# A two-block transformer trunk on one core: seven-product pairs in the last product, attention outputs kept on chip, the last two gate tiles plain

## The chip, the cores and the metric

One core of one Trainium2 chip runs the whole program. The metric is device time in microseconds (us), the median of the runs of one kernel; one further execution is profiled. TensorE (PE in the rows, with its weight loads as PEld) multiplies, VectorE (DVE) and ScalarE (ACT) do elementwise work, GpSimd (POOL) does elementwise work and issues software DMAs, SyncE (SP) issues most of the other DMAs.

## The reference, cut to what matters

Everything is f32 with 512 tokens and a model width of 2048. The first block has two layers; each is a norm, one wide input product, two kinds of attention side by side, a gate, an output product and a residual. The second block has one layer with 16 extra tokens ahead, a stick-breaking attention, a pooling branch, two sigmoid gates and an output product, and a last norm.

```python
for l in range(2):                                   # first block
    h = rmsnorm(x, attn_norm_g[l]);  proj = h @ w_in[l]
    ya = swa_attention(qa, ka, va, sinks) * silu(ga)    # 16 heads of 64, window 128
    yb = mla_attention(cq, ckv, kr, ...) * silu(gb)     # 8 heads, value width 128
    x = x + concat([ya, yb]) @ w_out[l]
x = rmsnorm(x, final_norm_g)
# second block, on meta tokens + x
zin = rmsnorm(x) @ w_in_2      # q, k, v, g_attn, u, g_pool, m_attn, m_pool
merged = sigmoid(m_attn) * (o_attn @ w_attn_up) + sigmoid(m_pool) * (o_pool @ w_pool_up)
out = rmsnorm(x + merged @ w_out_2)
```

## The kernel before, in words

Activations lie transposed: a tile is 128 features by 512 tokens, and a width of 2048 is 16 tiles. Each f32 operand is split into two fp32r parts, a high one (`split`, a ScalarE cast) and a low one (a VectorE subtraction, both in lines 133 to 139), and each product is three matmuls, high by high, high by low and low by high (`mm3`, line 152). The same is done to each weight block: `w_raw` (line 178) loads 128x1024 f32 by a DMA of SyncE into one of four `wr` buffers, and `load_w_split` (line 215) makes `wh` on ScalarE and `wl` on VectorE, three buffers each. `next_w` (line 222) keeps two split blocks ahead. A plain output tile takes two blocks and 96/2 = 48 matmuls of 512 columns. `run_gemm` (line 281) runs one tile, or a group of three, and calls `tick` after each step, which lets up to three side tasks (Python generators such as an attention head) put their instructions in between by a hand-kept clock (`clock`, line 141). The order of TensorE is that program order; the order of the other engines and the slots in memory are planned by the framework from modelled durations. All activation tiles share 74 slots (`NSLOT`, `slot`, line 108); an instruction that needs a slot waits until an earlier tile's last reader is done.

The gate columns of the second block, `ma` and `mp` (sixteen tiles each), use a scheme of seven products (`run_pair`, line 312): two output tiles are treated as a 2x2 block product of weights (four blocks a11, a12, a21, a22, and four sums of them) with half-width (256 tokens) right-hand sides, which are sums and differences of the activation tiles k and k+8 made by `t_set` (line 291). Seven half-width products of 24 matmuls each, 168 matmuls of 256 columns, replace 96 of 512. The weight sums are made earlier by GpSimd: `plan_sums` and `sum_step` (lines 191 to 208) issue eight DRAM-to-DRAM DMAs for each pair, some of them accumulating, into `wsd`, two for each three weight loads from the thirteenth load on; each waits for a matmul as its pace.

In each layer of the first block the order (`_order1`, line 46) is: low-rank inputs; then per pair of MLA heads its projections and gates (`gb`); then k, v, q and gate tiles of the windowed attention (`qa`, `ga`), with `swa_pair` (line 452) as a side task for each `qa`; then the output product with `w_out`, sixteen tiles, the first three as a group. The attention outputs y0 to y7 are the MLA heads, y8 to y15 the windowed pairs. `ydst` (line 754) stores y0 to y13 to DRAM through GpSimd's queue, and `yget` (line 760) loads them back through SyncE's queue and splits them: y0 to y7 after the gate tiles ga 4 to ga 7, the others when the output product first needs them.

In the second block the order (`_order2`, line 57) is: eight heads of k, q, v, gate; pooling tiles u, gp, pw; the gate pairs `ma`, `mp`; then sixteen times an `au` and a `pu` tile (48 plain matmuls together), whose right-hand sides are the sixteen attention and pooling outputs o0 to o15, loaded from DRAM by `o_load` (line 1110) after the last gate pair is issued; then the last product with `w_out2` on mg0 to mg15. There fourteen plain tiles (`finish`, line 1196) are followed by the last two tiles in two halves of 256 tokens, so that the final norm of the first half (`scale_out`, line 1219) overlaps the second half. All sixteen residual tiles `hs` stay on chip until then.

Of the kernel before, what the change touches and what calls it, by code (L numbers as in the profile page):

```python
# [37 lines left out]
GRP = 3  # L38
NSLOT = 74
HN = S // 2  # L40
SUMPAIRS = NC
NSIDE = 3
# [55 lines left out]
def trunk_kernel(ctx, tc, xT, w_in, w_qkv, w_out, w_in2, w_pool, w_aup, w_pup, w_out2, metaT, vec, cst, outT):  # L98
# [78 lines left out]

    def w_raw(src, n, tag="wr", bufs=4):
        raw = wp.tile([P, WCOLS], F32, tag=tag, name=tag, bufs=bufs)[:, :n]
        nc.sync.dma_start(raw, src)  # L180
        return raw
# [9 lines left out]
    def plan_sums(pairs):  # L191


        lists = []
        for p, (a11, a12, a21, a22) in enumerate(pairs):
            s1, s2, s3, s4 = (wsd[p, k] for k in range(4))
            lists.append([(s1, a21, 0), (s3, a11, 0), (s1, a22, 1), (s2, a11, 0), (s3, a21, 1), (s2, s1, 1),
                          (s4, a12, 0), (s4, s2, 1)])
        for p in range(0, len(lists), 2):
            for ops in zip(*lists[p:p + 2]):  # L200
                presum.extend(ops)

    def sum_step():
# [87 lines left out]
    def t_set(a, b):  # L291


        ra, rb = slot("ra"), slot("rb")
        tt(ra, f32(a[0]), f32(a[1]), ALU.add)
        tt(rb, f32(b[0]), f32(b[1]), ALU.add)
        b11, b12, b21, b22 = ra[:, :HN], ra[:, HN:], rb[:, :HN], rb[:, HN:]
# [119 lines left out]
    xd = [tc.dram_tile([P, NC, S], F32, name=f"xd{i}") for i in range(2)]  # L417
    yd = [tc.dram_tile([P, NC, S], F32, name=f"yd{i}") for i in range(2)]

# [32 lines left out]
    def swa_pair(i, qps, r, st, nsink, gate, ydst):  # L452
# [80 lines left out]
        nc.gpsimd.tensor_tensor(y, y, gate.pop(("a", i)), ALU.mult)  # L533
        ydst(8 + i, y)

# [75 lines left out]
    def mla_head(h, pr, kr, gate, ydst):  # L611
# [53 lines left out]
        tt(y, o, gate.pop(("b", h)), ALU.mult)  # L665
        ydst(h, y)

# [5 lines left out]
    def plan():  # L673
# [23 lines left out]
        for kind, i in SEQ2:  # L697
# [6 lines left out]
            elif kind in ("ma", "mp"):  # L704
                if i % 2 == 0:
                    blocks = (w_in2[t, 0], w_in2[t, 1], w_in2[t + 1, 0], w_in2[t + 1, 1])
                    wq.extend((src, WCOLS) for src in pair_steps(len(pairs), *blocks))
                    pairs.append(blocks)
                t += 1
            else:  # L710
                for u in range(2):
                    wq.append((w_in2[t, u], WCOLS))
                t += 1
        grouped(w_out2, 0, GRP)
        for j in list(range(GRP, NC)) + [NC - 2, NC - 1]:
            for u in range(2):
                wq.append((w_out2[j, u], WCOLS))

        plan_sums(pairs)
# [18 lines left out]
    def layer(lay, h, rd, x_src, x_dst):  # L738
# [14 lines left out]

        def ydst(c, t):
            if c < NC - 2:
                nc.gpsimd.dma_start(yd[lay][:, c, :], t)
                t = True
            y[c] = t

        def yget(c):  # L760
            if ys[c] is None:
                need(lambda: y[c] is not None)
                t = y[c]
                if t is True:
                    t = slot("yr")
                    nc.sync.dma_start(t, yd[lay][:, c, :])
                ys[c] = split(t, f"y{c}")
                y[c] = None
# [7 lines left out]
        for kind, i in SEQ1:  # L776
# [21 lines left out]
            elif kind == "pc":  # L798
                pr = proj.pop(i)
                mla_proj_c(st["ckvn"], pr)  # L800
                for hh in range(2):
                    start_side(mla_head(2 * i + hh, pr, kr, gate, ydst), 6000 + 3000 * hh)
            elif kind == "ka":
# [3 lines left out]
            elif kind == "qa":  # L807
                start_side(swa_pair(i, run_gemm(2, 8, hget), rd["r"], st, nsink, gate, ydst))
            elif kind == "ga":
                gate["a", i] = gate_silu(run_gemm(2, 8, hget), rd["r"], "ga")  # L810
                if i >= 4:
                    yget(2 * i - 8)
                    yget(2 * i - 7)

# [305 lines left out]
    for kind, i in SEQ2:  # L1120
# [21 lines left out]
        elif kind == "pw":  # L1142
            wh, wl = next_w()
            rhs = [pooled.pop(2 * i), pooled.pop(2 * i + 1)]
            for d in range(2):
# [6 lines left out]
                nc.sync.dma_start(od[:, SB + 2 * i + d, :], t)  # L1152
        elif kind in ("ma", "mp"):
            if i % 2:
                continue
            if not oo:
                need(lambda: len(done) == SB)
                oo = [None] * (2 * SB)
            at = i + (0 if kind == "ma" else NC)
            c = run_pair(tset, 8)  # L1160
            if (kind, i) == ("mp", NC - 2):
                X2 = tset = None
                for k in range(SB):
                    oo[k] = o_load(k)
            for d, t in enumerate(pair_out(c, sr)):
                nc.scalar.dma_start(sgd[:, at + d, :], gate_sigmoid(t, "sg"))
            if X2 is None:
                for k in range(SB, 2 * SB):
                    oo[k] = o_load(k)
        elif kind == "au":  # L1170
# [24 lines left out]

    def finish(j, ps, sl, n):

        hs = hss[j][:, sl]
        tt(hs, ps, hs, ALU.add)
        q = slot("oq", F32, n)  # L1200
        act(q, hs, AF.Square)
        nc.scalar.mul(hs, hs, vcol(V_FIN2 + j))
        return q

    full = slice(0, S)
    for j in range(NC - 2):
        hs_load(j)
        if j == 0:
            first = run_gemm(2, 8, mget, group=GRP)
        q = finish(j, first[j] if j < GRP else run_gemm(2, 8, mget), full, S)  # L1210
        if acc is None:
            acc = q
        else:
            nc.gpsimd.tensor_tensor(acc, acc, q, ALU.add)
    hs_load(NC - 2)
    hs_load(NC - 1)
    HS = S // 2

# [134 lines left out]
```

## Time and profile before

| | |
|---|---|
| median of 3 runs | 2760.93 us (2760.64 to 2765.09) |
| profiled execution | 2759.14 us |
| its span, first to last instruction | 2757.4 us |
| mean granted TensorE clock | 0.991 of full speed |
| TensorE busy | 2688.1 us (97%) |
| VectorE, ScalarE, GpSimd busy | 1605.9, 1217.0, 507.9 us |

The profile's busy time of TensorE counts a matmul until its modelled end, so it says little about how dense the stream is; the distance from one matmul's start to the next does. A stretch of the trace with a known number of matmuls of one width gives that distance, and a stretch that is longer than its matmuls need shows what was lost there.

### The profile page before, as it was taken

How to read it: one execution, taken by the hardware profiler on the slowest of the kernel's cores; microseconds unless marked ns; L12 is line 12 of the kernel's file. 1: busy time of each engine (PE TensorE's matmuls, PEld its weight loads, DVE VectorE, ACT ScalarE, POOL GpSimd, SP SyncE). 2: the span in 40 equal slices, each digit the busy share in tenths (PEclk: the TensorE clock that was granted, in tenths of full speed). 3: DMA queues.
4: the chain of work that ended last, by engine and by line, in shares of the span. 5: the costliest groups of instructions: out<-in, count | busy, mean ns of one | idle time of the engine just before them, and what ended most of it. 6: DMA issues, size and time to landing. Idle time of an engine off the chain costs nothing.

```text
span 2757.4 us, 37840 instructions
## 1 busy us (share of the span) xinstructions
PE 2688.1 (97%) x14809; PEld 2315.0 (84%) x14809; DVE 1605.9 (58%) x2399; ACT 1217.0 (44%) x2021; POOL 507.9 (18%) x461
## 2 busy tenths in 40 slices
PE   8999999899999999999999999999999999899997
PEld 6888888688788888877888989898899999688886
DVE  7767567544476756655554444547566666544445
ACT  5445455432344445553334433443346666422232
POOL 4121132222111213223411111111220000011112
PEclk9999999999999999999999999999999999999998
DMA  5354554567654554557632222223346666644334
GB/s 182 114 142 131 138 140 139 168 199 206 174 135 134 141 136 138 150 149 196 188 114 76 77 79 82 70 77 118 100 138 218 208 215 212 199 143 143 120 121 130
DMA packets 129410, 395.81 MB, mean 144 GB/s; under 512 B 14400, under 2 KB 18880, under 8 KB 129232
## 3 DMA queue, kind: packets, MB, share of 16 engines
q1 hardware_dynamic: 103568, 309.90, 35.1%
q0 software_dynamic: 20912, 75.04, 12.5%
q10 hardware_dynamic: 4752, 8.46, 0.8%
q8 instruction: 116, 1.90, 0.3%
q14 instruction: 62, 0.51, 0.1%
HBM read 360.84 MB, written 99.61 MB: 167 GB/s over the span
## 4 chain that ended last, share of the span: by engine, by line
PE 51%; issue 2%; DVE 2%; ACT 1%; POOL 1%; DMA 1%; SPq 0%; DVEq 0%; POOLq 0%; ACTq 0%
PE mm L146 27%; PE mmA L146 5%; PE y L146 5%; PE mmB L146 5%; PE x L146 3%; PE z L146 3%; ACT sp L129 1%; PE so L146 1%; POOL suf L989 0%; DMA ol<-od 0%; DVE out L1231 0%; POOL suf L988 0%; PE pw L146 0%; DVE sufl L122 0%; DMA yr<-yd 0%
## 5 line engine op out<-in xcount | busy, mean ns | idle before, releaser
L218 ACT CAST wh<-wr 128x1024 fp32r<-128x1024 f32 (+2 forms) x496 | 512.0, 1032 | 1001.0 <-PE mm L146 643.7
L122 DVE TENSOR_TENSOR wl<-wr,wh 128x1024 fp32r<-128x1024 f32 (+2 forms) x496 | 637.1, 1286 | 361.1 <-ACT wh L218 344.7
L146 PE MATMUL mm<-hh,wh 128*128 128x512 f32 x1024 | 410.7, 401 | 6.7 <-ACT wh L218 6.5
L146 PE MATMUL mm<-hh,wl 128*128 128x512 f32 x1024 | 405.6, 396 | 4.3 <-DVE wl L122 4.2
L146 PE MATMUL mm<-hl,wh 128*128 128x512 f32 x1024 | 405.6, 396 | 2.2 <-DVE hl L125 2.2
L146 PEld LDWEIGHTS mm<-hh,wl 128*128 128x128 f32 x1024 | 193.4, 189 | 50.3 <-DVE wl L122 5.8
L146 PEld LDWEIGHTS mm<-hh,wh 128*128 128x128 f32 x1024 | 193.8, 189 | 43.0 <-ACT wh L218 6.5
L146 PEld LDWEIGHTS mm<-hl,wh 128*128 128x128 f32 x1024 | 193.6, 189 | 39.8 <-DVE hl L125 4.0
L206 POOL DMA_DIRECT2D wsd<-in_w_in x96 | 62.7, 653 | 500.8 <-PE mm L146 339.6
L146 PE MATMUL mm<-Xh,wh 128*128 128x512 f32 x384 | 152.7, 398 | 0.0
L146 PE MATMUL mm<-Xl,wh 128*128 128x512 f32 x384 | 151.4, 394 | 0.0
L146 PE MATMUL mm<-Xh,wl 128*128 128x512 f32 x384 | 151.1, 394 | 0.0
L1178 POOL TENSOR_TENSOR ym<-ym,yp 128x512 f32<-128x512 f32 x16 | 21.7, 1354 | 489.0 <-DVE yp L122 391.6
L146 PE MATMUL mmA<-Xh,wh 128*128 128x264 f32 x384 | 109.9, 286 | 0.0
L146 PE MATMUL mmB<-Xh,wl 128*128 128x264 f32 x384 | 109.8, 286 | 0.0
L146 PE MATMUL mmB<-Xh,wh 128*128 128x264 f32 x384 | 109.7, 286 | 0.0
L146 PE MATMUL mmB<-Xl,wh 128*128 128x264 f32 x384 | 109.5, 285 | 0.0
L146 PE MATMUL mmA<-Xh,wl 128*128 128x264 f32 x384 | 109.3, 285 | 0.0
L146 PE MATMUL mmA<-Xl,wh 128*128 128x264 f32 x384 | 109.2, 284 | 0.0
L146 PEld LDWEIGHTS mm<-Xh,wl 128*128 128x128 f32 x384 | 72.1, 188 | 16.8
L131 ACT ACTIVATE p<-p,nm 128x256 f32<-128x256 f32 (+1 forms) x128 | 60.7, 475 | 57.6 <-DVE nm L486 56.4
L146 PEld LDWEIGHTS mm<-Xh,wh 128*128 128x128 f32 x384 | 72.2, 188 | 15.0
(874 smaller groups left out, 6951.0 us busy)
## 6 DMA issues: line engine op xcount, KB each, us to landing
wr<-in_w_in SPq DMA_DIRECT2D x272, 512.0 KB, 3.7
wr<-in_w_out SPq DMA_DIRECT2D x100, 512.0 KB, 3.8
wsd<-in_w_in POOLq DMA_DIRECT2D x96, 512.0 KB, 4.6
wr<-wsd SPq DMA_DIRECT2D x64, 512.0 KB, 4.3
wsd<-wsd POOLq DMA_DIRECT2D x32, 512.0 KB, 6.0
xd<-xn SPq DMA_DIRECT2D x32, 256.0 KB, 3.0
sgd<-sga ACTq DMA_DIRECT2D x32, 256.0 KB, 2.9
wr<-in_w_aup SPq DMA_DIRECT2D x16, 512.0 KB, 3.7
```

What stands on the lines that cost most here:

```text
L122: nc.vector.tensor_tensor(out, a, b, op)
L129: nc.scalar.activation(out, x, func, bias=bias, scale=scale)
L131: nc.scalar.activation(out, x, func, bias=bias, scale=scale, accum_out=accum_out)
L146: last_pe[0] = nc.tensor.matmul(out, a, b, start=start, stop=stop, skip_group_check=True).ins
L206: i = nc.gpsimd.dma_start(dst, src, **kw)
L218: nc.scalar.copy(hi, raw)
L1178: nc.gpsimd.tensor_tensor(ya, ya, yp, ALU.add)
```

## The change

- The last product: tiles 0 to 3 stay plain, tiles 4 to 13 become five seven-product pairs, tiles 14 and 15 stay plain in halves. The right-hand sums come from eight more `t_set`s, built by a side task while the first four tiles run. The output of a pair is added to `hs` by seven half-width operations instead of two full ones.
- `plan_sums` gets five more pairs from `w_out2` and loses one: 20 pairs for 16, so 160 summing DMAs for 128.
- The last two `mp` tiles are plain, so the t sets of the gates are released two plain tiles earlier; o0 to o7 are loaded ahead of the first of these tiles, o8 to o15 after it.
- y0 to y15 of both layers of the first block stay in slots; `yd` with its stores and loads goes. y0 to y7 are split one at a time ahead of qa 0 to qa 7.
- `NSLOT` rises from 74 to 80, the `wr` buffers fall from four to three.
- The first two additions of each `t_set` go from VectorE to GpSimd.
- The first eight `hs` tiles are stored to DRAM (`hsd`) by GpSimd's queue once they are done, and loaded back by SyncE's queue after the last pair.

```diff
@@ -36,9 +36,11 @@
 GRP = 3
-NSLOT = 74
+NSLOT = 80
 HN = S // 2
-SUMPAIRS = NC
+NPLAIN = 4
+NSPILL = 8
+SUMPAIRS = NC - 1 + (NC - 2 - 4) // 2
 NSIDE = 3
@@ -175,7 +177,7 @@
-    def w_raw(src, n, tag="wr", bufs=4):
+    def w_raw(src, n, tag="wr", bufs=3):
         raw = wp.tile([P, WCOLS], F32, tag=tag, name=tag, bufs=bufs)[:, :n]
@@ -199,6 +201,7 @@
                 presum.extend(ops)
+        assert len(lists) % 2 == 0 and len(lists) <= SUMPAIRS
@@ -292,8 +295,8 @@
         ra, rb = slot("ra"), slot("rb")
-        tt(ra, f32(a[0]), f32(a[1]), ALU.add)
-        tt(rb, f32(b[0]), f32(b[1]), ALU.add)
+        nc.gpsimd.tensor_tensor(ra, f32(a[0]), f32(a[1]), ALU.add)
+        nc.gpsimd.tensor_tensor(rb, f32(b[0]), f32(b[1]), ALU.add)
         b11, b12, b21, b22 = ra[:, :HN], ra[:, HN:], rb[:, :HN], rb[:, HN:]
@@ -415,7 +418,6 @@
     xd = [tc.dram_tile([P, NC, S], F32, name=f"xd{i}") for i in range(2)]
-    yd = [tc.dram_tile([P, NC, S], F32, name=f"yd{i}") for i in range(2)]
@@ -531,7 +533,7 @@
         nc.gpsimd.tensor_tensor(y, y, gate.pop(("a", i)), ALU.mult)
-        ydst(8 + i, y)
+        ydst[8 + i] = y
@@ -663,7 +665,7 @@
         tt(y, o, gate.pop(("b", h)), ALU.mult)
-        ydst(h, y)
+        ydst[h] = y
@@ -702,7 +704,10 @@
             elif kind in ("ma", "mp"):
-                if i % 2 == 0:
+                if (kind, i) >= ("mp", NC - 2):
+                    for u in range(2):
+                        wq.append((w_in2[t, u], WCOLS))
+                elif i % 2 == 0:
                     blocks = (w_in2[t, 0], w_in2[t, 1], w_in2[t + 1, 0], w_in2[t + 1, 1])
@@ -712,10 +717,16 @@
         grouped(w_out2, 0, GRP)
-        for j in list(range(GRP, NC)) + [NC - 2, NC - 1]:
+        for j in range(GRP, NPLAIN):
             for u in range(2):
                 wq.append((w_out2[j, u], WCOLS))
-
+        for j in range(NPLAIN, NC - 2, 2):
+            blocks = (w_out2[j, 0], w_out2[j, 1], w_out2[j + 1, 0], w_out2[j + 1, 1])
+            wq.extend((src, WCOLS) for src in pair_steps(len(pairs), *blocks))
+            pairs.append(blocks)
+        for j in [NC - 2, NC - 1] * 2:
+            for u in range(2):
+                wq.append((w_out2[j, u], WCOLS))
         plan_sums(pairs)
@@ -751,20 +762,10 @@
-        def ydst(c, t):
-            if c < NC - 2:
-                nc.gpsimd.dma_start(yd[lay][:, c, :], t)
-                t = True
-            y[c] = t
-
         def yget(c):
...
                 need(lambda: y[c] is not None)
-                t = y[c]
-                if t is True:
-                    t = slot("yr")
-                    nc.sync.dma_start(t, yd[lay][:, c, :])
-                ys[c] = split(t, f"y{c}")
+                ys[c] = split(y[c], f"y{c}")
                 y[c] = None
@@ -799,18 +800,16 @@
                 for hh in range(2):
-                    start_side(mla_head(2 * i + hh, pr, kr, gate, ydst), 6000 + 3000 * hh)
+                    start_side(mla_head(2 * i + hh, pr, kr, gate, y), 6000 + 3000 * hh)
             elif kind == "ka":
...
             elif kind == "qa":
-                start_side(swa_pair(i, run_gemm(2, 8, hget), rd["r"], st, nsink, gate, ydst))
+                yget(i)
+                start_side(swa_pair(i, run_gemm(2, 8, hget), rd["r"], st, nsink, gate, y))
             elif kind == "ga":
                 gate["a", i] = gate_silu(run_gemm(2, 8, hget), rd["r"], "ga")
-                if i >= 4:
-                    yget(2 * i - 8)
-                    yget(2 * i - 7)
@@ -1151,22 +1150,26 @@
         elif kind in ("ma", "mp"):
+            at = i + (0 if kind == "ma" else NC)
+            if (kind, i) >= ("mp", NC - 2):
+                if i == NC - 2:
+                    tset = None
+                    oo = [o_load(k) for k in range(SB)]
+                t = slot("sg")
+                tt(t, run_gemm(2, 8, x2), sr, ALU.mult)
+                nc.scalar.dma_start(sgd[:, at, :], gate_sigmoid(t, "sg"))
+                if i == NC - 2:
+                    oo += [o_load(k) for k in range(SB, 2 * SB)]
+                else:
+                    X2 = None
+                continue
             if i % 2:
                 continue
-            if not oo:
+            if (kind, i) == ("ma", 0):
                 need(lambda: len(done) == SB)
-                oo = [None] * (2 * SB)
-            at = i + (0 if kind == "ma" else NC)
             c = run_pair(tset, 8)
-            if (kind, i) == ("mp", NC - 2):
-                X2 = tset = None
-                for k in range(SB):
-                    oo[k] = o_load(k)
             for d, t in enumerate(pair_out(c, sr)):
                 nc.scalar.dma_start(sgd[:, at + d, :], gate_sigmoid(t, "sg"))
-            if X2 is None:
-                for k in range(SB, 2 * SB):
-                    oo[k] = o_load(k)
         elif kind == "au":
@@ -1193,28 +1196,66 @@
-    def finish(j, ps, sl, n):
-
-        hs = hss[j][:, sl]
-        tt(hs, ps, hs, ALU.add)
+    hsd = tc.dram_tile([P, NSPILL, S], F32, name="hsd")
+
+    def square_gain(j, hs, n):
         q = slot("oq", F32, n)
...
+    def finish(j, ps, sl, n):
+
+        hs = hss[j][:, sl]
+        tt(hs, ps, hs, ALU.add)
+        return square_gain(j, hs, n)
+
+    def tile_done(j, q):
+        if acc is not None:
+            nc.gpsimd.tensor_tensor(acc, acc, q, ALU.add)
+        if j < NSPILL:
+            nc.gpsimd.dma_start(hsd[:, j, :], hss[j])
+            hss[j] = None
+        return q if acc is None else acc
+
+    tset = []
+
+    def build():
+        for k in range(8):
+            tset.append(t_set(mg[k], mg[k + 8]))
+            yield 4000
+
+    start_side(build())
     full = slice(0, S)
-    for j in range(NC - 2):
+    lo, hi = slice(0, HN), slice(HN, S)
+    for j in range(NPLAIN):
         hs_load(j)
...
         q = finish(j, first[j] if j < GRP else run_gemm(2, 8, mget), full, S)
-        if acc is None:
-            acc = q
-        else:
-            nc.gpsimd.tensor_tensor(acc, acc, q, ALU.add)
+        acc = tile_done(j, q)
+    need(lambda: len(tset) == 8)
+    for j in range(NPLAIN, NC - 2, 2):
+        hs_load(j)
+        hs_load(j + 1)
+        c = run_pair(tset, 8)
+        tt(hss[j][:, lo], c[0], hss[j][:, lo], ALU.add)
+        for d, h, k, op in ((0, hi, 1, ALU.add), (1, lo, 2, ALU.subtract), (1, hi, 3, ALU.subtract)):
+            t = hss[j + d][:, h]
+            for at, (x, f) in enumerate(zip(c[k], (ALU.add, op))):
+                if f == ALU.add:
+                    tt(t, x, t, ALU.add)
+                else:
+                    tt(t, t, x, ALU.subtract)
+        for d in range(2):
+            acc = tile_done(j + d, square_gain(j + d, hss[j + d], S))
+    tset = None
+    for j in range(NSPILL):
+        hss[j] = slot("hs")
+        nc.sync.dma_start(hss[j], hsd[:, j, :])
     hs_load(NC - 2)
     hs_load(NC - 1)
-    HS = S // 2
+    HS = HN
...
         yield 2500
```

## Rows read from the trace of the kernel before

**Rows 1.** The page: busy us (share of span) by engine.
```profile
PE 2688.1 (97%) x14809; PEld 2315.0 (84%) x14809; DVE 1605.9 (58%) x2399; ACT 1217.0 (44%) x2021; POOL 507.9 (18%) x461
```
**Rows 2.** Five stretches: length, busy us (instructions) by engine, clock, DMA share, GB/s.
```profile
core 0: us, PE busy (x) PEld busy (x) DVE busy (x) ACT busy (x) POOL busy (x), PEclk, DMA share, GB/s
2100.00:2298.10 198.10, 198.10 (x1683) 198.10 (x1682) 133.59 (x170) 122.85 (x170) 0.00 (x0) 1.00 0.69 213
...
2577.00:2688.00 111.00, 111.00 (x481) 90.11 (x480) 49.66 (x42) 34.94 (x43) 17.33 (x10) 1.00 0.38 121
2364.00:2393.00 29.00, 18.37 (x45) 10.24 (x44) 15.31 (x24) 14.34 (x24) 0.00 (x0) 0.76 0.65 209
541.50:565.00 23.50, 18.97 (x69) 13.99 (x68) 10.29 (x13) 9.05 (x13) 2.40 (x3) 0.85 0.56 169
1238.00:1268.00 30.00, 25.58 (x97) 19.50 (x96) 13.86 (x18) 11.43 (x18) 4.86 (x4) 0.89 0.61 169
```
**Rows 3.** Waits of TensorE: for whom, us in total, times, longest.
```profile
PE o L146 <- DVE pTl L122: 6.9, 8, 1.0
...
PE mm L146 <- ACT y11h L137: 5.4, 2, 3.0
PE o L146 <- ACT pTh L137: 4.9, 2, 2.5
PE zA L146 <- DVE sufl L122: 4.7, 8, 0.6
...
PE o L146 <- DVE ya L122: 1.7, 7, 0.3
...
PE z L146 <- DVE t12l L122: 0.3, 1, 0.3
```
**Rows 4.** SyncE's queue in time, 539 to 546 us (start, us, what).
```profile
539.33 0.33 SPq L180 DMA_DIRECT2D wr<-in_w_out  x1
539.75 0.38 SPq L766 DMA_DIRECT2D yr<-yd  x1
544.88 0.33 SPq L180 DMA_DIRECT2D wr<-in_w_out  x1
545.30 1.33 SPq L766 DMA_DIRECT2D yr<-yd  x3
```
**Rows 5.** ScalarE in time, 527 to 529 us.
```profile
527.18 0.62 ACT L137 CAST y7h<-yr 128x512 fp32r<-128x512 f32 x1 [2.45 <-DMA yr<-yd]
527.71 0.85 ACT L137 CAST pTh<-tp 128x512 fp32r<-128x512 f32 x2
```
**Rows 6.** SyncE's queue in time, 2352 to 2386 us.
```profile
2352.26 0.42 SPq L1112 DMA_DIRECT2D ol<-od  x1
...
2366.28 2.81 SPq L1112 DMA_DIRECT2D ol<-od  x5
...
2379.97 4.44 SPq L1112 DMA_DIRECT2D ol<-od  x7
```
**Rows 7.** VectorE by shape, 2560 to 2713 us: count, busy us, mean ns, idle before.
```profile
L122 DVE TENSOR_TENSOR wl<-wr,wh 128x1024 fp32r<-128x1024 f32 x28 | 35.5, 1266 | 41.6 <-ACT wh L218 41.6
L125 DVE SCALAR_TENSOR_TENSOR hs<-hs,vecs,r 128x512 f32<-128x512 f32 x14 | 22.7, 1621 | 0.2 <-DMA hs<-xd 0.2
L122 DVE TENSOR_TENSOR hs<-mm,hs 128x512 f32<-128x512 f32 x13 | 9.0, 691 | 42.8 <-PE mm L146 42.8
```
**Rows 8.** Single tiles: ns min/median/max (`wl` of 2393 to 2560 us, a pair's drain `c`, `y0l`).
```profile
L122 DVE TENSOR_TENSOR wl<-wr,wh x30: 1224/1227/2354, 2394.5 to 2555.7; 128x1024 fp32r<-128x1024 f32 x30
L122 DVE TENSOR_TENSOR c<-ab,z x16: 412/422/423, 2063.7 to 2375.1; 128x256 f32<-128x256 f32 x16
L122 DVE TENSOR_TENSOR y0l<-yr,y0h x2: 1780/1781/1782, 452.3 to 1146.7; 128x512 fp32r<-128x512 f32 x2
```
**Rows 9.** Weight casts and DMA issues of 2046 to 2345 us (KB, median us to landing); the slowest class of the page.
```profile
L218 ACT CAST wh<-wr x106: 1030/1049/1054, 2046.0 to 2343.8; 128x1024 fp32r<-128x1024 f32 x106
wr<-wsd SPq DMA_DIRECT2D x61, 512.0 KB, 4.3
wr<-in_w_in SPq DMA_DIRECT2D x45, 512.0 KB, 4.3
...
wsd<-wsd POOLq DMA_DIRECT2D x32, 512.0 KB, 6.0
```
**Rows 10.** GpSimd: an addition of the page, `suf` of one head in time, sums of squares by shape.
```profile
L1178 POOL TENSOR_TENSOR ym<-ym,yp 128x512 f32<-128x512 f32 x16 | 21.7, 1354 | 489.0 <-DVE yp L122 391.6
1453.57 0.84 POOL L988 TENSOR_TENSOR suf<-sp 128x128 f32<-128x128 f32 x1 [12.13 <-DVE sp L125]
...
1458.31 0.62 POOL L989 COPY suf<-sp 128x128 f32<-128x128 f32 x1
L1214 POOL TENSOR_TENSOR oq<-oq 128x512 f32<-128x512 f32 x12 | 20.8, 1733 | 124.6 <-ACT oq L129 124.6
L206 POOL DMA_DIRECT2D wsd<-in_w_in x96 | 62.7, 653 | 500.8 <-PE mm L146 339.6
```
**Rows 11.** The chain that ended last: the first half's outputs.
```profile
2734.93 6.50 DVE out L1231 x11
```

## The prediction

> **What bounds the kernel now.** I read the page first, then the program cut into stretches, then TensorE's waits, and only then the single engines around each wait. The page says TensorE [rows 1], and the stretches say how dense it is. In the middle of the gate pairs 1683 matmuls start in 198.10 us; ten pairs are 1680, so a pair takes 19.81 us and a 256-column matmul 118 ns. In the last product 481 matmuls stand in 111.0 us; ten plain tiles are 480, so a tile takes 11.10 us and a 512-column matmul 231 ns [rows 2]. Both at a granted clock of 1.00. In those stretches nothing waits, and only a smaller number of columns can make them shorter.
>
> The rest is what TensorE waits for, and it sits in a few places [rows 3]. I price a place by its matmuls: count times 231 ns, taken from its length. At the start of the `au` and `pu` tiles 29.0 us hold 45 matmuls, which need 10.4: 18.6 us lost. At the start of the two output products of the first block 23.5 us hold 69 (15.9) and 30.0 us hold 97 (22.4): 7.6 and 7.6, so 15.2 lost. The granted clock in the three is 0.76, 0.85 and 0.89: after TensorE had stood still it ran for a time at 1.2 instead of 2.4 GHz, and that is inside these losses [rows 2]. Then single waits of the windowed attention: 4.9 us in two waits for `pTh`, 6.9 and 1.7 for `pTl` and `ya` [rows 3].
>
> **The change part by part.**
>
> Products. Two plain tiles are 22.20 us, a pair 19.81, so 2.39 less. Five pairs come in, one goes out: 4 x 2.39 = 9.6 us less [rows 2]. This needs nothing but that the pairs run as densely as in the gates.
>
> The `au` start. Before, the sixteen loads of o had to squeeze through slots that came free only as the last pair ended: the first was issued at 2352.26, five at 2366.28, seven at 2379.97 [rows 6], while `au` wanted o0 to o7 at about 2364. After, the t sets (32 slots) are free at the end of the last pair, two plain tiles earlier. Seven were issued in 4.4 us [rows 6], and with 4.3 for a landing (that of a weight block twice as large [rows 9]) eight need some 10 us; the first eight now have 22.2 us, the second eight 11.1 plus 5.5 for `au` 0, 16.6 us. Both fit. Bounds: all 18.6 back, or none if slots stay short; I take 2 left, since the need is met with 6 us to spare: 16.6 less. The other cost is that the last `mp` tile's gates are on ScalarE and VectorE at that time too; these engines are busy for half of that stretch [rows 2].
>
> The first block's outputs. Loads of y10 and y11 went out one by one, each right behind a weight load for which SyncE's queue had waited: 539.75 behind 539.33, 545.30 behind 544.88 [rows 4]; that is why TensorE waited for y10 and y11. With y in slots nothing is queued there, and y8 to y15 need only a cast and a subtraction (0.62 and 0.69 us each) while the group of three tiles runs its first half. Of 15.2 I leave 3. The wait for `pTh` (4.9) had the same cause: ScalarE stood 2.45 us at y7 for its load, with `pTh` queued behind it [rows 5]; I leave 1. The waits for `pTl` and `ya` (8.6) came at the six steps where two y were split ahead of them, with `y0l` stretched to 1.78 us, against 0.69 for an operation of the same size without company [rows 7, 8]. Now one y is split at each of sixteen steps; half the work at nearly three times the places. Bounds: nothing, and 16 x 1.43 = 23 us; I take 6, just under the old value. Together: 12.2 + 3.9 + 2.6 = 18.7 less. What these y cost is slots: at ga 7 the six that y8 to y13 did not hold before, which is what NSLOT gives; but from the first qa on eight are held that were free before. GpSimd loses 28 stores, in nobody's way.
>
> Three `wr` buffers. A buffer is held from the issue to the end of `wl`: 4.3 us landing, 1.05 cast, 1.23 subtraction [rows 9, 8], with the handovers about 6.8. Three of these may take three products, 3 x 2.83 = 8.49 us in a pair and 16.6 in plain tiles. So 0 is charged; `wl` at its longest, 2.35 [rows 8], gives 7.9, still inside. Bounds 0 and 6 us (single late landings). Behind a waiting weight load stand SyncE's other loads, `hs` and `ol`, but these are needed later than the weights.
>
> Thirty-two more summing DMAs. The plan is at the same pace, two in three loads, so it now runs 48 loads longer; the last 36 of them are those of four and a half heads of the second block, with 24 issues of 0.65 us on GpSimd, each behind its wait for a matmul. GpSimd makes `suf` there, a chain of 5.4 us in each head, and TensorE already waits for it at every head, 0.6 us [rows 10, 3]. Bounds 0 and 8 us (a few issues in each of the chains); I take 1.5.
>
> `t_set` additions on GpSimd. 1.35 us instead of 0.69, twice for each set [rows 10, 7]. Sets 0 to 6 of the gates have a tile or more to spare; the last was 0.3 us late before [rows 3]; I charge 0.5 (0 to 2). In the last product the eight sets have four tiles, 44.4 us; GpSimd needs 16 x 1.35 = 22 us and three or four sums of squares at 1.73 [rows 10]. Covered; if not, each us is one on TensorE.
>
> VectorE in the five pairs. Per pair: seven `wl` of 1.23, two `hs` scalings of 1.62, nine half-width operations of 0.42 [rows 7, 8]: 8.6 + 3.2 + 3.8 = 15.6 of 19.81 us, 79%; in the gates' pairs it was 67% [rows 2]. The bank that the next pair's second product overwrites is drained 2.83 us after the pair ends, which is room for three of these. I charge 2.0 (0 to 10) for the five pairs and the change-over.
>
> What GpSimd's additions do to VectorE shows in the rows: one `wl` in the `au` stretch took 2.35 us instead of 1.23, and the scaling of `hs`, next to the sums of squares, has a mean of 1.62 us [rows 8, 7]. The Trainium skill ("SBUF — State Buffer", "Who interferes with whom") says why, and it speaks against this change: a VectorE instruction with two inputs in SBUF and a GpSimd instruction that reads SBUF share one read port pair, and the second to start is blocked fully until the first is done. The trace agrees in direction; the wait seen is 1.12 us, near one addition of 1.35. By the rule every addition on GpSimd may cost VectorE one such block; its result is the second rival.
>
> Spilling `hs`. Eight stores are off the path (GpSimd's queue, no reader for tens of us). The eight loads, 256 KB each, wait for slots of the t sets, so most start when the last pair ends, and SyncE's weight loads stand behind those that wait. At the 213 GB/s of the gates' stretch 2.1 MB take 9.8 us [rows 2]; the first reader is the first half's outputs, after two half tiles of 5.65 us and the norm, some 13 us later. It fits narrowly. Charged 1.5 on TensorE (0 to 6) and 0.5 on the tail (0 to 4: outputs of the first half were 6.5 us of work [rows 11], hidden under the second half; what is late there comes out at the end).
>
> Sum: -9.6 - 16.6 - 18.7 + 1.5 + 0.5 + 2.0 + 1.5 + 0.5 = -38.9. Against the profiled execution, 2759.1 (span 2757.4), that is 2720.2; the median of the runs stands 1.8 above the profiled one, so 2722.
>
> **The rivals.**
> First: the waits of the first block only move. For: slots stay the limit (as many more held as given, and for longer), and one split at each of sixteen steps may cost as much as two at six. Against: no load stands in SyncE's queue any more. Then the 18.7 is not won: 2741.
> Second: VectorE becomes the bound of the five pairs. For: 79% by the sum, with casts, drains and scalings in one queue. If every `wl` and both scalings took their stretched time, 7 x 1.12 = 7.8 us come on top: 23.4 us a pair, 3.6 over, 18 us for five: 2740. Against: GpSimd works in a pair for two sums of squares, not for seven. This is also what the port rule would give in its worst case.
> Both together: 2759, no change.
> Third, slower: three `wr` buffers starve the seven-product stage. It decides at a hold of 8.49 us; from 9.3 on (0.28 us on each of the 140 products of 20 pairs) it eats the whole gain. With landings of 6.0, as the summing DMAs have [rows 9], and `wl` at 2.35, the hold is 9.6 and the price 140 x 0.37 = 52 us: 2774. Against: landings of 4.3 in that very stage, with nothing on GpSimd's queue there.
>
> **How the numbers follow.** Forecast 67% (2722), first rival 14%, second 8%, both together 5%, third 6%. The range reaches down to where everything waited for is regained and nothing is charged (-9.6 - 18.6 - 15.2 - 4.9 - 8.6 = -57, 2704) and up past the first two rivals with a little of the charges, 2747. A difference under 0.2% (5.5 us) can't be told from none here. Faster: forecast and the first two rivals, 89%; same: both together, 5%; slower: the third, 6%.
>
> **What would show it.** Right: pairs of 19.8 us in the last product; no wait of TensorE for y10, y11 or o8, and no dip of the granted clock at those places; TensorE's waits for `pTl` spread over more and shorter ones; the `wr` loads issued later but casts still released by TensorE, not by a DMA. Wrong: casts `wh` in the pairs released by a DMA (third rival); waits of z, x or y for VectorE (second); TensorE waiting for `suf` more than 0.6 us in the first heads; the outputs of the first half after the last matmul.

## The result and the profile after

The changed kernel takes 2722.48 us, the median of four runs (2720.21 to 2723.28), against 2762.76 us before, run beside it: a ratio of 0.9853, 95% interval 0.9836 to 0.9870. The forecast was 2722. Its total is right and three of its terms are not, and they cancel, as the rest of this document shows. Of the four runs of e10 below one took 6133.54 us, far from all others, and its ratio leaves that run out.

The page of the changed kernel (busy us, share of the span, instructions; then the loads of weight sums with KB each and median us to landing):

```profile
span 2720.5 us, 38463 instructions
...
PE 2666.5 (98%) x15097; PEld 2318.5 (85%) x15097; DVE 1652.7 (61%) x2472; ACT 1237.9 (46%) x2057; POOL 570.5 (21%) x505
...
wr<-wsd SPq DMA_DIRECT2D x80, 512.0 KB, 4.2
```

VectorE and GpSimd have more to do than in [rows 1], TensorE less. The stretches that answer to [rows 2], with two of the start of the last product (length, busy us and instructions by engine, granted clock, DMA share, GB/s):

```profile
534.00:557.50 23.50, 23.50 (x103) 19.06 (x102) 11.51 (x13) 8.88 (x11) 4.75 (x5) 1.00 0.73 227
1211.00:1241.00 30.00, 30.00 (x132) 24.39 (x131) 17.11 (x22) 11.62 (x18) 8.67 (x8) 1.00 0.69 184
2331.00:2360.00 29.00, 21.29 (x69) 14.15 (x68) 14.14 (x19) 14.28 (x22) 0.00 (x0) 0.76 0.47 158
2521.70:2575.50 53.80, 48.28 (x206) 38.43 (x205) 50.75 (x57) 18.26 (x26) 29.23 (x20) 0.97 0.30 95
2575.50:2581.00 5.50, 1.93 (x14) 1.53 (x14) 4.79 (x9) 3.70 (x6) 1.88 (x2) 1.00 0.32 91
2600.30:2679.40 79.10, 79.10 (x675) 79.10 (x674) 53.70 (x73) 41.98 (x53) 15.36 (x12) 1.00 0.72 227
```

The first two lie at the start of the output products of the first block: 103 and 132 matmuls where before there were 69 and 97, at a clock of 1.00. Nothing is lost there any more. The third, the start of the `au` tiles, has 69 matmuls in 29 us, before 45; at 231 ns each that is 16.0 us, so 13 are still lost, and the clock is again 0.76. The fourth and fifth are new losses: the first four tiles of the last product and the first half-width product behind them. In the fourth VectorE is busy for 50.75 of 53.8 us. The sixth holds the later pairs: 675 matmuls, four pairs, in 79.1 us, so 19.77 us a pair, as dense as the pairs of the gates.

TensorE's waits, which answer to [rows 3] (for whom, us in total, times, longest):

```profile
PE mm L148 <- DVE wl L124: 10.0, 5, 3.2
...
PE zA L148 <- DVE sufl L124: 4.6, 8, 0.6
PE mm L148 <- ACT o8h L139: 3.1, 1, 3.1
PE mm L148 <- ACT o6h L139: 2.7, 1, 2.7
...
PE z L148 <- DVE t12l L124: 2.2, 2, 1.7
PE z L148 <- ACT t12h L139: 1.9, 1, 1.9
PE mm L148 <- ACT o9h L139: 1.7, 1, 1.7
```

No y, no `pTh` and no `pTl` is left in the list. The waits for `wl` have grown from 4.2 us in two (the kernel before and e1 below have the same), those for the t sets (`t12h`, `t12l`) from 0.3.

For all kernels of this study I give one number by stage: for each matmul the distance to the next one's start, less 231 ns for 512 columns or 118 for 256 (109, 175 and 122 for 128, 384 and 264), summed. It is the time in which TensorE stood still or ran at the lower clock. Windowed attention and output products are those of both layers, without the norm behind the product; the last product includes the final norm of the first half. Each row comes from the profiled execution of its kernel alone.

| us lost by TensorE in | windowed attention | output products | gate tiles | au, pu | last product | median us |
|---|---|---|---|---|---|---|
| before | 12.9 | 24.6 | 0.6 | 19.1 | 3.1 | 2762.8 |
| after | 1.1 | 0.7 | 1.8 | 13.5 | 17.4 | 2722.5 |
| e1_before_slots | 12.5 | 22.2 | 0.7 | 17.5 | 3.0 | 2756.7 |
| e2_before_y | 1.1 | 0.7 | 1.8 | 17.3 | 3.1 | 2720.9 |
| e10_two_splits | 2.3 | 0.3 | 1.0 | 17.9 | 3.8 | 2722.7 |
| e3_plain_last | 1.1 | 0.7 | 1.9 | 14.1 | 3.2 | 2721.6 |
| e4_tset_dve | 1.1 | 0.7 | 2.2 | 13.7 | 17.9 | 2724.8 |
| e11_six_plain_pool | 1.1 | 0.7 | 1.8 | 13.5 | 12.7 | 2718.9 |
| e8_six_plain | 1.1 | 0.7 | 2.2 | 14.1 | 3.9 | 2712.9 |
| e7_o_pool | 1.1 | 0.7 | 1.8 | 6.9 | 17.2 | 2717.9 |
| e9_both | 1.1 | 0.7 | 2.2 | 8.4 | 4.9 | 2706.5 |
| e12_o_first | 1.1 | 0.7 | 2.2 | 4.6 | 3.8 | 2703.1 |

The span fell by 36.9 us. By the first two lines of the table: 35.7 less in the first block, 5.6 less at the `au` tiles, 14.3 more in the last product, 1.2 more in the gates; 9.6 less for the products; the rest, -1.5, is spread over the other stages and the tail.

### The profile page after: what moved, and what is told of

Same layout as the page of the kernel before. It is cut to its first block, busy times and chain, and to the rows that moved or that the text cites. A ratio compares the mean times of both kernels' runs of the same rounds, so it can differ in the third digit from the quotient of the medians.

```text
span 2720.5 us, 38463 instructions
## 1 busy us (share of the span) xinstructions
PE 2666.5 (98%) x15097; PEld 2318.5 (85%) x15097; DVE 1652.7 (61%) x2472; ACT 1237.9 (46%) x2057; POOL 570.5 (21%) x505
## 4 chain that ended last, share of the span: by engine, by line
PE 89%; DVE 5%; ACT 2%; issue 1%; POOL 1%; DMA 1%; SPq 0%; DVEq 0%; POOLq 0%; ACTq 0%
PE mm L148 53%; PE y L148 6%; PE mmB L148 5%; PE mmA L148 5%; PE x L148 4%; PE z L148 4%; PE msc L148 1%; PE qn L148 1%; DVE wl L124 1%; PE sc L148 1%; PE o L148 1%; PE mo L148 1%; PE tp L152 1%; PE kn L148 1%; ACT sp L131 1%
## 5 line engine op out<-in xcount | busy, mean ns | idle before, releaser
L221 ACT CAST wh<-wr 128x1024 fp32r<-128x1024 f32 (+2 forms) x508 | 524.5, 1033 | 900.7 <-PE mm L148 493.7
L124 DVE TENSOR_TENSOR wl<-wr,wh 128x1024 fp32r<-128x1024 f32 (+2 forms) x508 | 658.2, 1298 | 319.0 <-ACT wh L221 302.2
L148 PE MATMUL mm<-Xh,wh 128*128 128x512 f32 x416 | 165.0, 397 | 0.0
L148 PE MATMUL mm<-Xh,wl 128*128 128x512 f32 x416 | 163.9, 394 | 0.0
L148 PE MATMUL mm<-Xl,wh 128*128 128x512 f32 x416 | 163.6, 393 | 0.0
L148 PEld LDWEIGHTS mm<-Xh,wl 128*128 128x128 f32 x416 | 78.1, 188 | 18.1
L148 PEld LDWEIGHTS mm<-Xl,wh 128*128 128x128 f32 x416 | 78.2, 188 | 16.4
L148 PEld LDWEIGHTS mm<-Xh,wh 128*128 128x128 f32 x416 | 78.3, 188 | 16.1
```

The lines of the kernel that those rows point to most:

```text
L124: nc.vector.tensor_tensor(out, a, b, op)
L148: last_pe[0] = nc.tensor.matmul(out, a, b, start=start, stop=stop, skip_group_check=True).ins
L221: nc.scalar.copy(hi, raw)
```

## Experiments: the first block

**Slots alone.** The kernel before with the new memory plan and nothing else.

```diff
-NSLOT = 74
+NSLOT = 80
-    def w_raw(src, n, tag="wr", bufs=4):
+    def w_raw(src, n, tag="wr", bufs=3):
```

> The kernel before with 80 slots and three raw weight buffers, nothing else. The changed kernel lost 37.5 us less... that is, in its first block TensorE lost 1.8 us in all where the kernel before lost 37.5 us (windowed attention and start of the output product, both layers). Theory A: those losses came from the loads of y that stood behind weight loads in SyncE's queue. Then more slots alone leave most of them: at least 25 us still lost, time 2750 to 2765 us. Rival B: they came from slots that were not free, and six more slots are the cure: first-block losses under 12 us, time 2725 to 2740 us. Rival C: three raw buffers cost time by themselves: time above 2765 us, with casts released by a DMA in the seven-product stage.

Measured: 2756.67 us, ratio to before 0.9993 (0.9984 to 1.0002). The first block loses 34.7 us, against 37.5 before; TensorE's waits in this kernel:

```profile
PE o L146 <- DVE pTl L122: 6.9, 8, 1.0
...
PE o L146 <- ACT pTh L137: 4.7, 2, 2.4
...
PE mm L146 <- ACT o8h L137: 4.5, 1, 4.5
PE mm L146 <- ACT y11h L137: 4.5, 2, 2.7
PE mm L146 <- DVE wl L122: 4.2, 2, 3.2
PE mm L146 <- ACT y10h L137: 3.9, 2, 2.3
```

Compared with [rows 3] hardly a wait has changed. So six slots are not the cure. Three raw buffers cost nothing either: the gate pairs lose 0.7 us, as before. That settles the third rival on the side of the forecast.

**y on chip alone.** The run above, with `yget` and the heads as in the changed kernel.

```diff
-            if c < NC - 2:
-                nc.gpsimd.dma_start(yd[lay][:, c, :], t)
...
-                    nc.sync.dma_start(t, yd[lay][:, c, :])
...
+                yget(i)
                 start_side(swa_pair(...))
-                if i >= 4:
-                    yget(2 * i - 8)
-                    yget(2 * i - 7)
```

> As the run before it, and the attention outputs of both layers kept on chip, with one split ahead of each qa tile; gates and last product as in the kernel before. Theory A: the first block alone gives 34 to 37 us, time 2724 to 2730 us, with no wait of TensorE for y10, y11 or pTh. Rival: the gain needs the other parts too (a different plan of the whole program), then less than 25 us, time above 2736 us. The start of the au tiles should still lose 15 to 20 us.

Measured: 2720.88 us, ratio 0.9860 (0.9845 to 0.9874); 1.8 us lost in the first block. This part alone is as fast as the whole change. That is 3 us below the range that theory A gave, and far from the rival's. The run takes the stores of y away together with the loads. But SyncE's queue of the kernel before, in 440 to 550 us, shows no load of y waiting for a store: its loads (L766) waited 0.9 us in all, for TensorE, and the weight loads ahead of them 97.1.

```profile
SPq L180 <- DVE wl L122: 97.1, 15, 9.2
SPq L766 <- PE tp L150: 0.6, 1, 0.6
```

**Two splits at a time.** The same, with y0 to y7 split two at a time after ga 4 to ga 7, as in the kernel before.

```diff
-                yget(i)
...
+                if i >= 4:
+                    yget(2 * i - 8)
+                    yget(2 * i - 7)
```

> The kernel before with 80 slots, three raw weight buffers and y kept on chip, as in the run of that name, but y0 to y7 are split two at a time after ga 4 to ga 7, as in the kernel before. That tells where the 10.6 us of waits for pTl and ya went. Theory: they came from two splits ahead of the pair's own casts; then they come back, 5 us a layer, and the time is 2729 to 2733 us. Rival: they came from the loads (a cast that waits for a load holds the queue); then it is 2719 to 2723 us, as with one split at a time.

Measured: 2722.66 us, ratio 0.9864 (0.9849 to 0.9879). The windowed attention loses 2.3 us instead of 12.9. My theory fell, the rival holds: the waits for `pTl` and `ya` did not come from two splits standing together but from the loads. ScalarE and VectorE take their instructions in the planned order, so a split whose y has yet to land, or was placed late because of it, holds the pair's own casts. VectorE at `ga` 4 of the first layer, before (three lines) and in this run (the last):

```profile
454.70 1.23 DVE L122 TENSOR_TENSOR wl<-wr,wh 128x1024 fp32r<-128x1024 f32 x1 [0.58 <-ACT wh L218]
455.84 0.69 DVE L122 TENSOR_TENSOR y1l<-yr,y1h 128x512 fp32r<-128x512 f32 x1
457.87 1.29 DVE L122 TENSOR_TENSOR pTl<-tp,pTh 128x512 fp32r<-128x512 f32 x2
```

```profile
451.34 0.69 DVE L122 TENSOR_TENSOR y1l<-yb,y1h 128x512 fp32r<-128x512 f32 x1
```

The split of y1 has moved from right ahead of the pair's own work to 4.5 us earlier. The stretched `y0l`, 1.78 us in the kernel before and 0.69 here, was not it: behind it VectorE stood idle for 0.58 us. The order of the splits is worth 1.2 us.

## Experiments: the last product

**Plain throughout.** The changed kernel with fourteen plain tiles, without t sets, spill and weight sums for them.

```diff
-        for j in range(GRP, NPLAIN):
+        for j in range(GRP, NC - 2):
...
-    start_side(build())
...
-    for j in range(NPLAIN, NC - 2, 2):
-        ...
-        c = run_pair(tset, 8)
```

> The changed kernel with its last product plain throughout (no t sets there, no spill of hs, fifteen pairs' weight sums instead of twenty); everything else as changed. Five pairs save 5 x 2.39 = 12.0 us of matmuls, but the last product of the changed kernel loses 17.4 us against 3.1 before. Theory: what the pairs save there is given back by the t sets and the change-over, so this kernel takes 2719 to 2723 us, no slower than the changed one, with the last product at 183 us long. Rival, the pairs are worth their matmuls: 2730 to 2735 us.

Measured: 2721.6 us, ratio 0.9863 (0.9848 to 0.9878), no slower than the changed kernel; the last product is 182.6 us long against 184.8 with the pairs. The five pairs save 12.0 us of matmuls and lose 14.2.

Where they lose it, two engines of the changed kernel show at the start of the product (start, us, what). VectorE:

```profile
2525.04 1.79 DVE L124 TENSOR_TENSOR mg15l<-ym,mg15h 128x512 fp32r<-128x512 f32 x1
2526.76 1.51 DVE L124 TENSOR_TENSOR t<-ra 128x256 f32<-128x256 f32 x1
...
2539.08 2.29 DVE L124 TENSOR_TENSOR wl<-wr,wh 128x1024 fp32r<-128x1024 f32 x1
...
2548.24 0.41 DVE L124 TENSOR_TENSOR t<-ra,rb 128x256 f32<-128x256 f32 x1
```

GpSimd in the same time:

```profile
2523.99 2.29 POOL L298 TENSOR_TENSOR ra<-mg0h,mg0l 128x512 f32<-128x512 f32 x1
...
2545.34 1.49 POOL L299 TENSOR_TENSOR rb<-mg14h,mg14l 128x512 f32<-128x512 f32 x1
2567.95 0.61 POOL L1217 DMA_DIRECT2D hsd<-hs  x1 [21.12 <-ACT hs L1204]
...
2571.92 1.30 POOL L298 TENSOR_TENSOR ra<-mg7h,mg7l 128x512 f32<-128x512 f32 x1
```

While GpSimd adds, from 2524 to 2547 us, a half-width operation of VectorE takes 1.51 us; right after, 0.41. The weight split due in that time starts at 2539.08, behind a row of t set operations, and TensorE waits for it. And the eighth set's additions stand behind the first spill store, for which GpSimd had waited 21.12 us; TensorE waits for this set at the first pair.

**Additions on VectorE.** The changed kernel with one edit:

```diff
-        nc.gpsimd.tensor_tensor(ra, f32(a[0]), f32(a[1]), ALU.add)
-        nc.gpsimd.tensor_tensor(rb, f32(b[0]), f32(b[1]), ALU.add)
+        tt(ra, f32(a[0]), f32(a[1]), ALU.add)
+        tt(rb, f32(b[0]), f32(b[1]), ALU.add)
```

> The changed kernel with the first two additions of each t set on VectorE again. Theory: in 2523 to 2547 us VectorE's half-width operations took 1.50 us instead of 0.42 while GpSimd did these additions, which delayed the weight splits (2.6 + 2.8 us of waits) and the last t set (4.0 us). Then this kernel loses 6 to 10 us less in the last product: 2713 to 2717 us. Rival, VectorE has too much work in that stretch whoever adds: the additions cost it 16 x 0.69 = 11 us more, same waits, 2720 to 2726 us. In the gate stage the first z waits no more than 0.6 us in either.

Measured: 2724.78 us, ratio 0.9876 (0.9860 to 0.9893), no faster; 17.9 us lost. Half of the theory held: the waits for weight splits in the first tiles are gone, and VectorE's operations take 0.41 us there. But TensorE waits in one piece for the eighth set:

```profile
PE z L148 <- ACT t12h L139: 9.9, 1, 9.9
```

VectorE of this kernel in time, ahead of that:

```profile
2574.69 0.75 DVE L127 SCALAR_TENSOR_TENSOR hs<-hs,vecs,r 128x512 f32<-128x512 f32 x1 [3.53 <-DMA hs<-xd]
2575.48 0.69 DVE L124 TENSOR_TENSOR hs<-mm,hs 128x512 f32<-128x512 f32 x1
2576.09 0.68 DVE L124 TENSOR_TENSOR ra<-mg7h,mg7l 128x512 f32<-128x512 f32 x1
```

The seventh set was done at 2565; the additions of the eighth (mg7) stand on VectorE behind the `hs` of a tile whose load it waits for. The additions moved, and what they had hidden came out in their place.

**Six plain tiles, four pairs**, first with the additions left on GpSimd, then on VectorE.

```diff
-NPLAIN = 4
+NPLAIN = 6
```

> The changed kernel with six plain tiles and four pairs in the last product; the additions of the t sets stay on GpSimd. It splits the two edits that stood together in the run with six plain tiles, where 3.9 us were lost in the last product. Theory: the eighth set is cured by the two more plain tiles alone, and GpSimd's additions cost the two late weight splits (2.6 and 2.8 us) and the lower clock behind them; then 8 to 11 us are lost there, time 2714 to 2718 us. Rival: with more time ahead of the first pair nothing of it matters, loss 5 us or less, time 2709 to 2713 us.

> The changed kernel with six plain tiles and four pairs in the last product instead of four and five, and the first two additions of each t set on VectorE. With these additions on VectorE and five pairs the last product still lost 17.9 us, 11 of them at the first pair, waiting for the eighth t set. Theory: that set waits for memory that comes free only when the first hs tiles are finished and stored, some 45 us after the product starts; 22 us more of plain tiles cover it. Then the loss falls to 3 to 6 us, against one pair less (2.4 us): 2709 to 2713 us. Rival: the eighth set is tied to the first pair's start (it waits for whatever comes free last), the loss stays at 10 us or more: 2719 to 2726 us.

Measured: 2718.92 us (0.9842, 0.9826 to 0.9859) with the additions on GpSimd, 12.7 us lost: more than I had expected, though the first pair waits for no set now. And 2712.90 us (0.9826, 0.9813 to 0.9840) with them on VectorE, 3.9 us lost. So of the loss of 14.3 us some 4.7 was the eighth set and some 9 GpSimd's additions, weight splits and the lower clock behind them; each hides a part of the other, which is why either edit alone gives little, and why these two prices hold in this order only: with five pairs, the additions on VectorE gave nothing. What keeps the eighth set back, a slot or the plan's order, these runs don't tell apart: two more plain tiles cover both.

## Experiments: the start of the au tiles

SyncE's queue of the changed kernel (start, us, what) shows why the earlier loads of o came to little; the second fence is what that queue waited for in 2305 to 2352 us:

```profile
2316.25 0.33 SPq L182 DMA_DIRECT2D wr<-in_w_aup  x1
2316.64 0.45 SPq L1111 DMA_DIRECT2D ol<-od  x1
2321.83 0.33 SPq L182 DMA_DIRECT2D wr<-in_w_pup  x1
2322.22 0.90 SPq L1111 DMA_DIRECT2D ol<-od  x2
...
2342.85 3.82 SPq L1111 DMA_DIRECT2D ol<-od  x7
```

```profile
SPq L182 <- DVE wl L124: 32.5, 8, 7.6
SPq L182 <- DMA sgd<-sga: 3.1, 1, 3.1
```

Every load of o goes out right behind a weight load that had waited for its buffer; none of them waits itself. In the kernel before it was the same queue [rows 6]: in 2345 to 2392 us the weight loads waited 27.8 us, the loads of o themselves 1.7, of which the longest is the second line.

```profile
SPq L180 <- DVE wl L122: 27.8, 9, 10.4
SPq L1112 <- DMA wr<-in_w_pup: 1.0, 1, 1.0
```

**Another queue for o.**

```diff
         t = slot("ol")
-        nc.sync.dma_start(t, od[:, c, :])
+        nc.gpsimd.dma_start(t, od[:, c, :])
```

> The changed kernel with the loads of o0 to o15 issued from GpSimd's queue instead of SyncE's; nothing else. In the changed kernel no load of o waits for a slot, but each stands in SyncE's queue behind a weight load that waits for its buffer (32.5 us in eight waits of 2305 to 2352), and TensorE loses 13.5 us at the start of the au tiles. Theory: the queue is the cause; then that loss falls to 0 to 4 us and the time to 2709 to 2714 us. Rival: the slots of the t sets come free too late anyway (the loads only move to another waiting queue), loss 10 us or more, time 2719 to 2724 us.

Measured: 6.9 us lost instead of 13.5, between theory and rival; 2717.92 us, ratio 0.9845 (0.9832 to 0.9859). The single runs spread from 2712.65, the profiled one, to 2721.0, so by time alone it can't be told from the changed kernel; the trace of the profiled run tells where the gain is, and the next run bears it out in time. All sixteen loads had landed at 2320, seven us before the first `au` tile. What is left, in TensorE's waits of this run, is o8:

```profile
PE mm L148 <- ACT o8h L139: 4.6, 1, 4.6
```

**Both**, the six plain tiles with VectorE's additions and o on GpSimd's queue:

> The two runs before it in one kernel. If both causes are as thought, their gains add: 2697 to 2704 us. If the loads of o on GpSimd's queue disturb what follows (t sets, weights), it ends above 2707 us.

Measured: 2706.53 us, ratio 0.9805 (0.9792 to 0.9819). The gains nearly add in the table (8.4 and 4.9 us lost, 6.9 and 3.9 in the two runs apart); the time is 6.4 us less than with the six plain tiles alone, and 2.5 us above the range. ScalarE of this run in time:

```profile
2333.22 1.04 ACT L221 CAST wh<-wr 128x1024 fp32r<-128x1024 f32 x1 [2.95 <-PE mm L148]
2334.17 0.62 ACT L131 ACTIVATE sga<-sg 128x512 f32<-128x512 f32 x1
2334.83 1.29 ACT L131 ACTIVATE sga<-sga 128x512 f32<-128x512 f32 x2
2336.88 0.63 ACT L131 ACTIVATE sga<-sga 128x512 f32<-128x512 f32 x1 [0.76 <-DVE sga L127]
2337.42 0.60 ACT L139 CAST o8h<-ol 128x512 fp32r<-128x512 f32 x1
```

The cast of o8, whose data has been there for long, stands behind a gate that nobody needs soon.

**o8 to o15 ahead of that gate** in the program:

```diff
-                t = slot("sg")
-                tt(t, run_gemm(2, 8, x2), sr, ALU.mult)
-                nc.scalar.dma_start(sgd[:, at, :], gate_sigmoid(t, "sg"))
+                ps = run_gemm(2, 8, x2)
                 if i == NC - 2:
                     oo += [o_load(k) for k in range(SB, 2 * SB)]
-                else:
+                t = slot("sg")
+                tt(t, ps, sr, ALU.mult)
+                nc.scalar.dma_start(sgd[:, at, :], gate_sigmoid(t, "sg"))
+                if i == NC - 1:
                     X2 = None
```

> The run with six plain tiles, additions on VectorE and the loads of o on GpSimd's queue, with the second eight loads of o and their splits put ahead of the gate of the first plain mp tile in program order. There all sixteen loads had landed before the au tiles began, and still TensorE waited 4.7 us for o8, whose cast stood on ScalarE behind that tile's gate and a weight cast that waits for TensorE. Theory: the order on ScalarE is what is left; then the loss at the au start falls from 8.4 to 2 to 5 us and the time to 2700 to 2704 us. Rival: the slots of the split parts are free only when the last gate tile has run, the loss stays at 7 us or more, 2705 to 2709 us.

Measured: 2703.12 us, ratio 0.9786 (0.9772 to 0.9801), 4.6 us lost, the wait for o8 at 1.4 us. The order on ScalarE was it. This kernel is faster than both kernels of the case, by 19 us than the changed one.

## Why the prediction came out right, point by point

**Products** (-9.6): as forecast. Pairs in the last product take 19.77 us, those of the gates 19.81 before and 19.87 after. The step is right by its own reading of the rows.

**The first block** (-18.7 forecast, -35.7 measured). The mechanism was right: loads queued behind weight loads; e1 and e2 separate it from the slots. The size was off in two ways. What could be won was priced at 28.7 us, from two cut-out stretches and a few waits; stage by stage it is 37.5, since the table of waits counts less than the distance between two starts of matmuls shows (1.0 and 1.24 us for a wait for `pTl`), and the time at the lower clock reaches beyond the stretches I cut (1.6 us at 1224 to 1228). And I left 10 of it: 6 of these for the splits, "half the work at nearly three times the places". e10 shows that two splits together were never the price.

**The `au` start** (-16.6 forecast, -5.6 measured). The failed step is "both fit". It compared the time from free slots to need with the time that eight loads take, and left out the queue, which the forecast had named in its next paragraph as the cause for y. [rows 6] had the loads in lots some 14 us apart; I took that for slots coming free. e7 and e12 show two queues in a row: SyncE's, then ScalarE's.

**The last product** (charged 2.0 and 1.5, measured 14.3). The failed step is "covered" for the t sets. It summed GpSimd's own time, 22 of 44 us, but not what VectorE's share becomes at three times its length, nor that the weight splits stand in the same queue. The pairs themselves, where I looked for trouble, had none: VectorE is busy 53.70 of 79.10 us, 68%, not 79%, as the scaling of `hs` takes 0.75 us when no sum of squares runs beside it, not the 1.62 of [rows 7]. GpSimd's additions mattered in another place than I had put them, at the making of the t sets: an operation of VectorE fell from 1.51 us beside them to 0.41 after them, and with six plain tiles, where the eighth set is no longer late, e8 against e11 prices them at 8.8 us of TensorE's time. The trace agrees there with the rule on the shared port that the forecast cites from the Trainium skill ("SBUF — State Buffer", "Who interferes with whom").

**Charged at little or nothing.** Three `wr` buffers: 0 by e1. In the last pairs three casts were released by a DMA, after 5.6 us in all, without a wait of TensorE. Summing in the heads: 1.5 charged, nothing seen; the wait for `suf` is 4.6 us in eight, before 4.7. The gates' first pair: 0.5 charged, and 0.2 measured, 20.61 us from its start to the next one's against 20.43. The 1.2 us of the table are for the whole stage: the other pairs take 19.87 instead of 19.81, as they do in e2 (19.89), where nothing of the t sets was changed; why is open. The spill's loads and the tail: 2.0 charged together; the loads went out at 2678.6 to 2683.7, and the time from the last matmul to the end fell from 14.7 to 14.0 us. TensorE waited 0.9 us for a weight split at 2693.

In sum the first block gave 17.0 us more than forecast, the `au` start 11.0 less, the last product cost 10.8 more, and the small terms gave 2.8 back: 36.9 us of the profiled execution instead of 38.9. The 2 us are made up by the last step of the forecast: the median stood 1.8 us above the profiled run before, and stands 0.2 above it now. The total was right by cancelling.

## What to carry to other kernels

A load that is ready to go gains little from an earlier place in the program if its queue has a waiting instruction ahead of it: read for each queue who stands in front, SyncE's first, then the engine that consumes the load. When a sum fits an engine's time, look at the stretch in which it falls and at what shares that engine's order and its port, above all the short work that TensorE waits for. And test the parts one at a time: here one of them gave the whole gain, and the one that saved matmuls was worth nothing until two other things were mended.

## What the runs showed of the hardware

After TensorE had stood still for a few us at the `au` start, the mean granted clock of 29 us was 0.76, before and after alike: a part of them at full speed (2.4 GHz) and a part, as here in the changed kernel, at half (1.2 GHz).

```profile
2342.00:2346.00 4.00, 2.02 (x3) 0.79 (x3) 1.69 (x3) 2.10 (x4) 0.00 (x0) 0.50 0.61 197
2346.00:2350.00 4.00, 2.71 (x5) 1.24 (x5) 1.55 (x3) 1.85 (x3) 0.00 (x0) 0.50 0.96 318
```

So 13 us were lost where the waits for o add up to 7.7. In e12 these waits are 2.2 us and the loss 4.6: 5.5 us less waiting gave 8.9. The gain of curing a wait was larger than the wait.

A VectorE operation of 128x256 with both inputs in memory took 1.51 us while GpSimd added tiles beside it and 0.41 otherwise, 3.7 times as long; one of 128x512 1.79 instead of 0.68. In that stream of additions each operation took about 1.1 us longer, whatever its size: a split of weights, 1.22 us alone, took 2.29. An addition of GpSimd takes 1.30 us alone and 1.46 to 2.29 in that stretch. The extra time is not always 1.1: once two additions in a row (2571.92 and 2573.17) stood beside one scaling of `hs`, and it took 3.41 us, where it takes 0.75 alone.

```profile
2571.61 3.41 DVE L127 SCALAR_TENSOR_TENSOR hs<-hs,vecs,r 128x512 f32<-128x512 f32 x1 [1.40 <-DMA hs<-xd]
2573.17 1.30 POOL L299 TENSOR_TENSOR rb<-mg15h,mg15l 128x512 f32<-128x512 f32 x1
```
